# Seven-product gated feed-forward: a PSUM copy put ahead of three activations, and further buffers for weights and their sums

## The chip, the cores and the metric

The kernel runs on one core of a Trainium2 chip. The metric is device time in microseconds of one execution, and less is better. The times of the kernel before are 1887.44, 1888.04 and 1890.42 us, median 1888.04 us.

## What the kernel computes

The reference is one hybrid decoder block over 1024 tokens of width 1024, in float32. Two token mixers (an RWKV-7 recurrence and a retention) run first; then comes the gated feed-forward, which is the part that the change touches:

```
def conv_ffn(h, w_up, conv_w, conv_b, w_down):
    u = h @ w_up                                  # 1024 -> 2 * 2816
    up = jnp.pad(u, ((0, 0), (CONV_WIDTH - 1, 0), (0, 0)))
    u = sum(up[:, i:i + T] * conv_w[i] for i in range(CONV_WIDTH)) + conv_b
    gate, val = jnp.split(u, 2, axis=-1)
    return (jax.nn.gelu(gate, approximate=True) * val) @ w_down
```

## The kernel before

Everything lies transposed, channels on the 128 partitions and tokens along the free dimension, in two halves of 512 tokens. The 2816 gate channels and the 2816 value channels are 22 pairs of tiles of 128. Every float32 product is made of three TensorE passes over operands split in a high and a low part (`mm3`, L224 to L226).

The first three pairs are done in the usual way (`up_std`). The other 19, the loop over `n`, use a scheme of seven products instead of eight: sums and differences of weight quarters (`sa`, and `st1`, `st2` written over) times sums of activations prepared before (`T1` to `T4`). For n below 4 (`NEAR`) two of the seven products were made earlier and come by DMA; from n = 4 on all seven are made in the loop, in TensorE's order: first half of the first product (X1, into `pX`), Z1 (`pZ`), T1 (`pT`), Y (`pY`), second half of the first product onto the same bank (X2), Z2 onto `pZ`, T2 onto `pT`. Each is four tiles by three passes, 12 matmuls, so 84 an iteration. Below, X1, X2 and so on mean these products; the order on TensorE runs across iterations, so that X1, Z1, T1 and Y of the next iteration stand behind X2, Z2, T2 of this one.

ACT copies X1 out of `pX` into `s1` (L1188), and X2 must wait for that, because it accumulates on the same bank. Other results: L1193 copies Z1 to `s5`, DVE adds T1 and Y (L1195, L1197), ACT copies X2 (L1200), POOL adds `s1` and `s5` (L1201), DVE adds Z2 and T2 (L1203, L1205). They fill `ub[0]` (gate channels) and `ub[1]` (value channels), each with two token halves.

Then `conv` runs four times an iteration (two tiles, two halves): one ACT activation (L1065) and two DVE operations with three operands (L1066, L1068). `gate` runs twice: a gelu on ACT (L1073), a DVE product (L1074), and a store to `f_d` issued from ACT's queue (L1075), which stands in that queue until the product is done.

The weights of an iteration: two loads from SP's queue (L1150, L1153) into `st1` and `st2`, each of two buffers that alternate; DVE makes `sa` in its single buffer (L1168, L1169) and two more differences in place (L1171, L1172); `cut` casts to the high part on ACT (L1164) and subtracts for the low part on POOL or DVE (L1165): for `w1`, `w2`, and both halves of `w3` on POOL, for half of `w4` on DVE. This code stands under a priority of 500 instructions, so it runs ahead of the products it serves.

A scheduler at compile time fixes each engine's order from a simulated timeline, by data readiness and program order, which `tc.high_priority(offset=...)` moves forward by so many instructions. On the chip every engine takes its list in order and waits on semaphores.

Of the kernel before, what the change touches and what calls it, by code (L numbers as in the profile page):

```python
# [9 lines left out]
F32 = mybir.dt.float32  # L10
F32R = mybir.dt.float32r
I32 = mybir.dt.int32
AF = mybir.ActivationFunctionType
# [15 lines left out]
E05 = math.exp(-0.5)  # L29
TWO_PI = 2.0 * math.pi  # L30
WPRIO = 500
MAGIC = 12582912.0
C1 = 6.25
C2 = 0.033203125
# [124 lines left out]
def body(tc, nc, xT, xN, pos, wch, wbrw, wbret, wout, wup, wdn, w2a2, gw2, rows, vecs, consts0, consts1, out):  # L159
    V, S, G, PE = nc.vector, nc.scalar, nc.gpsimd, nc.tensor  # L160
    ctx = ExitStack()

    @contextmanager
    def tile_pool(**kw):
        with tc.tile_pool(**kw) as pool:
            yield Lines(pool)

    with ctx:
# [7 lines left out]
        wp = ctx.enter_context(tile_pool(name="wp", bufs=3, reuse_waits="tile"))  # L176
# [25 lines left out]
        def load_w(src, kt, full=None, hi=None, lo=None, st=None, eng=None):  # L202

            wp, nb = wpools[cnt[0] % len(wpools)]
            with tc.high_priority(offset=WPRIO if cnt[0] > 3 else 0):
                if st is None:
                    st = wp.tile([128, full or kt, 128], F32, tag="ws", name="w_st", bufs=nb[0])[:, 0:kt, :]
                nc.sync.dma_start(st, src)
            with tc.high_priority(offset=WPRIO if cnt[0] > 1 else 0):
                if hi is None:  # L210
# [55 lines left out]
        ws = pz.tile([128, 2, KT, 128], F32, tag="ARp", name="w_sx")  # L266
        wx = pz.tile([128, 2, KT, 128], F32R, tag="BKp", name="w_x")
# [7 lines left out]
        with tile_pool(name="x0", bufs=2, reuse_waits="tile") as xp:  # L275
# [22 lines left out]
            for q in range(NJ):  # L298
                xn = xp.tile([128, D], F32, tag="xn", name="xn", bufs=3)
                nc.sync.dma_start(xn, xN[128 * q:128 * q + 128, :])  # L300
                S.activation(xn, xn, AF.Square, accum_out=rsm[:, q:q + 1])
            with tc.high_priority(offset=WPRIO):
                V.tensor_scalar(rsm[:, 8:16], rsm[:, 0:8], 1.0 / D, RMS_EPS, ALU.mult, ALU.add)
# [24 lines left out]
        with pctx, tile_pool(name="p1", bufs=1, reuse_waits="tile", side="right") as p1:  # L328
# [159 lines left out]
            n = gp.tile([128, 512], F32, tag="rt", name="nrot", bufs=1)  # L488
            V.tensor_scalar(n, ang, 1.0 / TWO_PI, C("turn"), ALU.mult, ALU.add)
            V.tensor_scalar(n, n, MAGIC, MAGIC, ALU.add, ALU.subtract)  # L490
            for c_ in (C1, C2, C3):
# [14 lines left out]
        def qk_pair(m):  # L506

            ws = [load_w(wch[14 + 2 * m + e], 8) for e in range(2)]
            for hf in range(2):
                h_ = slice(hf * 512, (hf + 1) * 512)  # L510
                ab = []
                for e in range(2):
                    ps = psA.tile([128, 512], F32, tag="a", name="ps_side")
                    proj(ws[e], ps, hf)
                    with tc.high_priority(offset=WPRIO):
                        t = gp.tile([128, 512], F32, tag=f"qk{e}", name="qk", bufs=1)
# [17 lines left out]
        def side_tile(i):  # L534

            w = load_w(wch[i], 8)
            for hf in range(2):
                ps = psA.tile([128, 512], F32, tag="a", name="ps_side")
                proj(w, ps, hf)
                with tc.high_priority(offset=WPRIO):  # L540
                    ot = gp.tile([128, 512], F32, tag="ot", name="ot")
# [237 lines left out]
        def first_stage(j):  # L779

            nonlocal R
            tk = slice(j * 128, (j + 1) * 128)
            with tc.high_priority(offset=WPRIO):
                zvg = t2.tile([128, 24, 128], F32, name="zvg")
# [181 lines left out]
        with (tile_pool(name="mg", bufs=2, reuse_waits="tile") as mp,  # L966
              tile_pool(name="mg2", bufs=1, reuse_waits="tile") as mp2):
            for hf in range(2):
# [43 lines left out]
                for cs_ in ((0, 1),) + tuple((c,) for c in range(2, 8)):  # L1012

                    ws = [load_w(wout[c], 8) for c in cs_]
# [30 lines left out]
        w3s = w3ctx.enter_context(tile_pool(name="w3s", bufs=1, reuse_waits="tile"))  # L1045
# [15 lines left out]
        def conv(pool, ub, b, j, src):  # L1061

            i = j + FT * b
            u = pool.tile([128, 512], F32, tag=f"u{b}", name="u_f")
            S.activation(u, src, AF.Identity, bias=VC("cb")[:, i:i + 1], scale=VC("cw2")[:, i:i + 1])  # L1065
            V.scalar_tensor_tensor(out=u, in0=ub[:, 1:513], scalar=VC("cw1")[:, i:i + 1], in1=u,  # L1066
                                   op0=ALU.mult, op1=ALU.add)
            V.scalar_tensor_tensor(out=u, in0=ub[:, 0:512], scalar=VC("cw0")[:, i:i + 1], in1=u,  # L1068
                                   op0=ALU.mult, op1=ALU.add)
            return u  # L1070

        def gate(j, hf, u0, u1):
            S.activation(u0, u0, AF.Gelu_apprx_tanh)  # L1073
            V.tensor_tensor(out=u0, in0=u0, in1=u1, op=ALU.mult)  # L1074
            nc.scalar.dma_start(f_d[hf, j], u0)  # L1075

# [33 lines left out]
        for n0 in range(0, NEAR, 2):  # L1110
            ws = [load_w(wup[NSTD + n], 8) for n in (n0, n0 + 1)]
# [27 lines left out]
        wx = ctx.enter_context(tile_pool(name="wx", bufs=1, reuse_waits="tile", side="right"))  # L1139
# [3 lines left out]
        fp = fctx.enter_context(tile_pool(name="fp", bufs=2, reuse_waits="tile"))  # L1143
        W8 = [128, 8, 128]
        lh, rh_ = slice(0, 4), slice(4, 8)

        for n, j in enumerate(range(NSTD, FT)):
            with tc.high_priority(offset=WPRIO):
                st1 = wp.tile(W8, F32, tag="ws", name="w_st", bufs=2)
                nc.sync.dma_start(st1, wup[j])  # L1150

                st2 = wx.tile(W8, F32, tag="ws", name="w_st", bufs=2) if n else w3s.tile(W8, F32, tag="ws", name="w_st")
                nc.sync.dma_start(st2, wup[j + FT])  # L1153
                sa = wx.tile(W8, F32, tag="sa", name="w_sa") if n else w3s.tile(W8, F32, tag="wh", name="w_sa")
                if n >= NEAR:
                    w1 = wp.tile(W8, F32R, tag="wh", name="w_hi", bufs=3), wx.tile(W8, F32R, tag="wl", name="w_lo", bufs=3)
                wh = (wx, 2) if n else (wp, 3)
                w2 = (wh[0].tile(W8, F32R, tag="wh", name="w_hi", bufs=wh[1]),
                      wx.tile(W8, F32R, tag="wl", name="w_lo", bufs=3) if n else w3s.tile(W8, F32R, tag="wl", name="w_lo"))
                w3 = wp.tile(W8, F32R, tag="wh", name="w_hi", bufs=3), wp.tile(W8, F32R, tag="wl", name="w_lo", bufs=2)  # L1160
                w4 = wh[0].tile(W8, F32R, tag="wh", name="w_hi", bufs=wh[1]), wp.tile(W8, F32R, tag="wl", name="w_lo", bufs=2)

                def cut(w, ks, src, eng):
                    S.copy(w[0][:, ks, :], src)  # L1164
                    eng.tensor_tensor(out=w[1][:, ks, :], in0=src, in1=w[0][:, ks, :], op=ALU.subtract)  # L1165
                if n >= NEAR:
                    cut(w1, slice(0, 8), st1, G)
                V.tensor_tensor(out=sa[:, lh, :], in0=st2[:, lh, :], in1=st2[:, rh_, :], op=ALU.add)  # L1168
                V.tensor_tensor(out=sa[:, rh_, :], in0=st1[:, lh, :], in1=st2[:, lh, :], op=ALU.subtract)  # L1169
                cut(w2, slice(0, 8), sa, G)  # L1170
                V.tensor_tensor(out=st2[:, lh, :], in0=sa[:, lh, :], in1=st1[:, lh, :], op=ALU.subtract)  # L1171
                V.tensor_tensor(out=st1[:, rh_, :], in0=st1[:, rh_, :], in1=st2[:, lh, :], op=ALU.subtract)  # L1172
                cut(w3, lh, st2[:, lh, :], G)
                cut(w3, rh_, st1[:, rh_, :], G)
                cut(w4, lh, st2[:, rh_, :], V)
            if n >= NEAR:
                pX = psA.tile([128, 512], F32, tag="a", name="ps_x")
            pZ = bank("ps_z", "B")
            pT = bank("ps_t", "CY"[n % 2])
            pY = bank("ps_y", "AI"[n % 2])  # L1180
            ub = [fp.tile([128, 1026], F32, tag=f"ub{b}", name="ub") for b in range(2)]
            for b in range(2):
                G.memset(ub[b][:, 0:2], 0.0)
            s1 = fp.tile([128, 512], F32, name="s1")
            s5 = fp.tile([128, 512], F32, name="s5")
            if n >= NEAR:
                mmb(pX, w1, range(4), hn2[0][0:4], True, True)
                S.copy(s1, pX)  # L1188
            else:
                nc.sync.dma_start(s1, e_d[n, 0])  # L1190
                nc.sync.dma_start(ub[0][:, 2:514], e_d[n, 1])
            mmb(pZ, w2, range(4), T1, True, True)
            S.copy(s5, pZ)  # L1193
            mmb(pT, w2, range(4, 8), T3, True, True)
            V.tensor_tensor(out=s5, in0=pT, in1=s5, op=ALU.add)  # L1195
            mmb(pY, w3, range(4), T2, True, True)
            V.tensor_tensor(out=s1, in0=pY, in1=s1, op=ALU.add)  # L1197
            if n >= NEAR:
                mmb(pX, w1, range(4, 8), hn2[0][4:8], False, True)
                S.copy(ub[0][:, 2:514], pX)  # L1200
            G.tensor_tensor(out=ub[1][:, 514:1026], in0=s1, in1=s5, op=ALU.add)  # L1201
            mmb(pZ, w3, range(4, 8), hn2[1][4:8], False, True)
            V.tensor_tensor(out=ub[0][:, 514:1026], in0=pZ, in1=s1, op=ALU.add)  # L1203
            mmb(pT, w4, range(4), T4, False, True)
            V.tensor_tensor(out=ub[1][:, 2:514], in0=pT, in1=s1, op=ALU.add)  # L1205
            for hf in range(2):
                cv = [conv(fp, ub[b][:, 512 * hf:512 * hf + 514], b, j, ub[b][:, 512 * hf + 2:512 * hf + 514])
                      for b in range(2)]
                gate(j, hf, *cv)
        fctx.close()  # L1210
        w3ctx.close()

# [68 lines left out]
        for c in range(8):  # L1281
# [5 lines left out]
            ws = [load_w(wdn[c][:, k0:k0 + kn, :], kn, full=8) for k0, kn in ((0, 8), (8, 8), (16, 6))]  # L1287
# [28 lines left out]
```

## Time and profile before

| quantity | value |
|---|---|
| median of three runs | 1888.04 us |
| the profiled execution's own time | 1895.04 us |
| its span | 1893.2 us |
| TensorE busy, share of the span | 94% |
| DVE, ACT, POOL busy | 62%, 34%, 36% |
| mean granted TensorE clock | 0.982 |
| iterations n = 4 to 18, from the first X2 to the last | 1322.53 to 1609.74 us |

The profile comes from one execution, with times from the start of its span. A busy time counts what an engine executes, also while an instruction stands blocked inside it; "idle before" is the time in which the engine waited ahead of an instruction, with the instruction that released it.

### The profile page before, as it was taken

Reading aid. Unit: us, or ns where it says so; the run is one execution under the profiler, and the core shown is the slowest. Engines: PE = TensorE matmul, PEld = TensorE weight load, DVE = VectorE, ACT = ScalarE, POOL = GpSimd, SP = SyncE. Lnnn points to the kernel's source line nnn. Section 1 sums busy time; section 2 is a strip of 40 time slices with the busy share of each in tenths; the row PEclk is TensorE's granted clock in tenths of the full one; section 3 lists DMA queues with packets and bytes.
Section 4 is the critical chain, followed back from the end, with each engine's and each line's share of the span. In section 5 each row is a group of like instructions: output and inputs, shape, how many; then the busy total and the mean of one; then the engine's idle time right before and its main releaser. Section 6 shows DMA issues by size and latency. Waiting matters only on the chain.

```text
span 1893.2 us, 27391 instructions
## 1 busy us (share of the span) xinstructions
PE 1786.2 (94%) x10610; PEld 1448.0 (76%) x10610; DVE 1182.6 (62%) x2068; ACT 649.9 (34%) x993; POOL 687.0 (36%) x491
## 2 busy tenths in 40 slices
PE   8779999999999999999999999888999999989996
PEld 7667778788777788888788778676777777868885
DVE  4786584755666634663444837789888887753413
ACT  6543211111111113322343435544434444443320
POOL 1344523311122122111463744554554454222523
PEclk9989999999999999999999999999999999999998
DMA  8233532433423225555653835433222222665531
GB/s 287 86 114 100 186 86 70 134 90 89 115 88 115 72 84 159 176 178 167 205 167 102 261 116 168 167 117 99 85 78 72 86 69 88 218 205 144 188 92 45
DMA packets 202690, 244.44 MB, mean 129 GB/s; under 512 B 60992, under 2 KB 136256, under 8 KB 201536
## 3 DMA queue, kind: packets, MB, share of 16 engines
q1 hardware_dynamic: 125712, 171.11, 29.8%
q10 hardware_dynamic: 76848, 71.59, 11.6%
q8 instruction: 83, 1.36, 0.3%
q14 instruction: 47, 0.39, 0.1%
HBM read 177.10 MB, written 65.54 MB: 128 GB/s over the span
## 4 chain that ended last, share of the span: by engine, by line
PE 53%; DVE 18%; DMA 8%; issue 4%; POOL 3%; ACT 3%; ACTq 0%; SPq 0%; DVEq 0%; POOLq 0%
PE ps_side L225 7%; PE ps_side L224 7%; PE ps_side L226 7%; DVE u_f L1066 4%; PE ps_dn L226 3%; PE ps_dn L225 3%; PE ps_dn L224 3%; DMA w_st<-in_wup_dram 2%; DVE u_f L1068 2%; POOL w_lo L1165 2%; DVE w_sa L1169 2%; PE ps_o L225 1%; PE ps_o L226 1%; PE ps_o L224 1%; DVE w_sa L1168 1%
## 5 line engine op out<-in xcount | busy, mean ns | idle before, releaser
L218 POOL TENSOR_TENSOR w_lo<-w_st,w_hi 128x1024 fp32r<-128x1024 f32 (+2 forms) x111 | 259.8, 2341 | 515.7 <-ACT w_hi L212 183.5
L212 ACT CAST w_hi<-w_st 128x1024 fp32r<-128x1024 f32 (+2 forms) x162 | 161.7, 999 | 412.6 <-PE ps_side L225 130.7
L225 PE MATMUL ps_side<-hnl,w_hi 128*128 128x512 f32 x640 | 256.2, 400 | 0.0
L224 PE MATMUL ps_side<-hnh,w_hi 128*128 128x512 f32 x640 | 255.6, 399 | 0.0
L226 PE MATMUL ps_side<-hnh,w_lo 128*128 128x512 f32 x640 | 254.9, 398 | 0.0
L224 PEld LDWEIGHTS ps_side<-hnh,w_hi 128*128 128x128 f32 x640 | 121.0, 189 | 26.9 <-issue 1.5
L225 PEld LDWEIGHTS ps_side<-hnl,w_hi 128*128 128x128 f32 x640 | 121.0, 189 | 26.5 <-issue 1.5
L226 PEld LDWEIGHTS ps_side<-hnh,w_lo 128*128 128x128 f32 x640 | 121.1, 189 | 26.3 <-issue 0.8
L218 DVE TENSOR_TENSOR w_lo<-w_st,w_hi 128x1024 fp32r<-128x1024 f32 (+1 forms) x51 | 65.2, 1279 | 82.3 <-ACT w_hi L212 40.6
L1066 DVE SCALAR_TENSOR_TENSOR u_f<-ub,vct,u_f 128x512 f32<-128x512 f32 x88 | 102.1, 1164 | 13.2 <-ACT u_f L1065 11.5
L1165 POOL TENSOR_TENSOR w_lo<-w_st,w_hi 128x512 fp32r<-128x512 f32 (+1 forms) x53 | 105.5, 2012 | 3.8 <-ACT w_hi L1164 2.3
L1065 ACT ACTIVATE u_f<-ub,vct 128x512 f32<-128x512 f32 x76 | 59.8, 812 | 124.4 <-DVE ub L1203 99.2
L224 PE MATMUL ps_rw<-hnh,w_hi 128*128 128x512 f32 (+1 forms) x224 | 87.7, 392 | 13.1 <-ACT hnh L289 6.8
L225 PE MATMUL ps_rw<-hnl,w_hi 128*128 128x512 f32 (+1 forms) x224 | 86.7, 387 | 0.5 <-DVE hnl L290 0.5
L226 PE MATMUL ps_rw<-hnh,w_lo 128*128 128x512 f32 (+1 forms) x208 | 80.0, 385 | 0.0
L226 PE MATMUL ps_b<-y_hi,w_lo 128*128 128x512 f32 x192 | 75.2, 392 | 2.8 <-DVE w_lo L218 1.8
L1068 DVE SCALAR_TENSOR_TENSOR u_f<-ub,vct,u_f 128x512 f32<-128x512 f32 x88 | 76.9, 892 | 0.2
L224 PE MATMUL ps_b<-y_hi,w_hi 128*128 128x512 f32 x192 | 75.2, 392 | 0.7 <-ACT w_hi L212 0.6
L225 PE MATMUL ps_b<-y_lo,w_hi 128*128 128x512 f32 x192 | 74.9, 390 | 0.0
L224 PE MATMUL ps_dn<-f_k,w_hi 128*128 128x512 f32 (+1 forms) x198 | 72.4, 366 | 0.0
L226 PE MATMUL ps_dn<-f_k,w_lo 128*128 128x512 f32 (+1 forms) x198 | 72.4, 366 | 0.0
L225 PE MATMUL ps_dn<-f_k,w_hi 128*128 128x512 f32 (+1 forms) x198 | 72.2, 366 | 0.0
(418 smaller groups left out, 4346.6 us busy)
## 6 DMA issues: line engine op xcount, KB each, us to landing
w_st<-in_wup_dram SPq DMA_DIRECT2D x54, 512.0 KB, 3.5
w_st<-in_wch_dram SPq DMA_DIRECT2D x52, 512.0 KB, 3.9
w_st<-in_wdn_dram SPq DMA_DIRECT2D x38, 512.0 KB, 4.0
pj_d<-ot ACTq DMA_DIRECT2D x64, 256.0 KB, 2.2
zvg<-pj_d SPq DMA_DIRECT2D x8, 1536.0 KB, 8.9
f_d<-u_f ACTq DMA_DIRECT2D x44, 256.0 KB, 2.1
L<-L_d SPq DMA_DIRECT2D x8, 1344.0 KB, 5.9
w_st<-in_wbret_dram SPq DMA_DIRECT2D x16, 512.0 KB, 3.9
```

The costliest lines, as they stand in the source:

```text
L212: S.copy(hi, st)
L218: eng.tensor_tensor(out=lo, in0=st, in1=hi, op=ALU.subtract)
L224: PE.matmul(ps, wh, xh, start=first and a == 0, stop=False, skip_group_check=skip)
L225: PE.matmul(ps, wh, xl, start=False, stop=False, skip_group_check=skip)
L226: PE.matmul(ps, wl, xh, start=False, stop=last and a == n - 1, skip_group_check=skip)
L1065: S.activation(u, src, AF.Identity, bias=VC("cb")[:, i:i + 1], scale=VC("cw2")[:, i:i + 1])
L1066: V.scalar_tensor_tensor(out=u, in0=ub[:, 1:513], scalar=VC("cw1")[:, i:i + 1], in1=u, op0=ALU.mult, op1=ALU.add)
L1068: V.scalar_tensor_tensor(out=u, in0=ub[:, 0:512], scalar=VC("cw0")[:, i:i + 1], in1=u, op0=ALU.mult, op1=ALU.add)
L1165: eng.tensor_tensor(out=w[1][:, ks, :], in0=src, in1=w[0][:, ks, :], op=ALU.subtract)
L1168: V.tensor_tensor(out=sa[:, lh, :], in0=st2[:, lh, :], in1=st2[:, rh_, :], op=ALU.add)
L1169: V.tensor_tensor(out=sa[:, rh_, :], in0=st1[:, lh, :], in1=st2[:, lh, :], op=ALU.subtract)
```

## The change

Two things change in the loop over `n`. First, buffers that the first stage of the feed-forward left free (the pool `w3s`) are used again: `st1` and `st2` take every third iteration's tile from there, so each rotates over three buffers, and `sa` alternates between two. Second, an iteration's last work is cut out into a function, `rest`: `conv` of both halves of the value tile, the gelu of the second half of the gate tile, both products and both stores. It is called in the next iteration, right behind the copy of X1 (for n of 4 and above), with `tc.issue_after`, which holds the block's ACT instructions behind that copy in ACT's list, and with a priority of 40. `conv` of both halves of the gate tile and the gelu of the first half stay where they were.

```
-                st1 = wp.tile(W8, F32, tag="ws", name="w_st", bufs=2)
+                st1 = (wp.tile(W8, F32, tag="ws", name="w_st", bufs=2) if n % 3 or not n else
+                       w3s.tile(W8, F32, tag="wl", name="w_st"))
...
-                st2 = wx.tile(W8, F32, tag="ws", name="w_st", bufs=2) if n else w3s.tile(W8, F32, tag="ws", name="w_st")
+                st2 = (wx.tile(W8, F32, tag="ws", name="w_st", bufs=2) if n % 3 else
+                       w3s.tile(W8, F32, tag="ws", name="w_st"))
...
-                sa = wx.tile(W8, F32, tag="sa", name="w_sa") if n else w3s.tile(W8, F32, tag="wh", name="w_sa")
+                sa = wx.tile(W8, F32, tag="sa", name="w_sa") if n % 2 else w3s.tile(W8, F32, tag="wh", name="w_sa")
...
                 mmb(pX, w1, range(4), hn2[0][0:4], True, True)
-                S.copy(s1, pX)
+                c1 = S.copy(s1, pX)
+                with tc.issue_after(c1.ins), tc.high_priority(offset=GPRIO):
+                    rest()
             else:
+                rest()
                 nc.sync.dma_start(s1, e_d[n, 0])
...
-            for hf in range(2):
-                cv = [conv(fp, ub[b][:, 512 * hf:512 * hf + 514], b, j, ub[b][:, 512 * hf + 2:512 * hf + 514])
-                      for b in range(2)]
-                gate(j, hf, *cv)
+            def part(b, hf, j=j, ub=ub):
+                return conv(fp, ub[b][:, 512 * hf:512 * hf + 514], b, j, ub[b][:, 512 * hf + 2:512 * hf + 514])
+            u0 = [part(0, hf) for hf in range(2)]
+            S.activation(u0[0], u0[0], AF.Gelu_apprx_tanh)
+            def rest(j=j, part=part, u0=u0):
+                gate(j, 0, u0[0], part(1, 0), gelu=False)
+                gate(j, 1, u0[1], part(1, 1))
+        rest()
```

## Rows read from the trace of the kernel before

**Rows 1.** Windows, twelve iterations: length, busy us of PE, PEld, DVE, ACT, POOL, clock, DMA.
```profile
1343.49:1589.81 246.32, 232.18 (x1009) 188.28 (x1009) 209.57 (x229) 110.08 (x169) 120.67 (x84) 1.00 0.24 77
```

**Rows 2.** The waits of PE from 1240 to 1660 us: us in total, times, longest.
```profile
PE ps_x L224 <- ACT s L1188: 18.4, 15, 2.5
PE ps_z L224 <- ACT s L1193: 3.3, 1, 3.3
```

**Rows 3.** The timeline of PE: start, us, what, [idle before <-releaser]; single matmuls.
```profile
1322.53 0.50 PE L224 MATMUL ps_x<-b_hi,w_hi 128*128 128x512 f32 x1 [2.51 <-ACT s L1188]
...
1410.57 0.39 PE L224 MATMUL ps_t<-b_hi,w_hi 128*128 128x512 f32 x1
...
1419.41 0.39 PE L224 MATMUL ps_t<-b_hi,w_hi 128*128 128x512 f32 x1
...
1609.74 0.50 PE L224 MATMUL ps_x<-b_hi,w_hi 128*128 128x512 f32 x1 [0.56 <-ACT s L1188]
```

**Rows 4.** The timeline of ACT through one iteration.
```profile
1400.17 0.81 ACT L1065 ACTIVATE u_f<-ub,vct 128x512 f32<-128x512 f32 x1 [7.81 <-DVE ub L1203]
...
1402.41 1.52 ACT L1065 ACTIVATE u_f<-ub,vct 128x512 f32<-128x512 f32 x2 [0.39 <-DVE ub L1205]
1403.84 0.61 ACT L1073 ACTIVATE u_f<-u_f 128x512 f32<-128x512 f32 x1
1404.36 0.56 ACT L1188 COPY s<-ps_x 128x512 f32<-128x512 f32 x1
...
1408.67 1.05 ACT L1164 CAST w_hi<-w_sa 128x1024 fp32r<-128x1024 f32 x1 [3.26 <-DVE u_f L1074]
```

**Rows 5.** The timeline of DVE through the same iteration.
```profile
1399.46 0.68 DVE L1203 TENSOR_TENSOR ub<-ps_z,s 128x512 f32<-128x512 f32 x1
...
1405.48 1.41 DVE L1068 SCALAR_TENSOR_TENSOR u_f<-ub,vct,u_f 128x512 f32<-128x512 f32 x2
...
1406.80 1.29 DVE L1074 TENSOR_TENSOR u_f<-u_f 128x512 f32<-128x512 f32 x2
...
1408.01 0.69 DVE L1195 TENSOR_TENSOR s<-ps_t,s 128x512 f32<-128x512 f32 x1
...
1408.61 0.69 DVE L1197 TENSOR_TENSOR s<-ps_y,s 128x512 f32<-128x512 f32 x1
...
1412.24 1.76 DVE L1168 TENSOR_TENSOR w_sa<-w_st 128x512 f32<-128x512 f32 x1 [2.95 <-POOL w_lo L1165]
...
1417.32 2.88 DVE L1066 SCALAR_TENSOR_TENSOR u_f<-ub,vct,u_f 128x512 f32<-128x512 f32 x1
1420.12 0.68 DVE L1203 TENSOR_TENSOR ub<-ps_z,s 128x512 f32<-128x512 f32 x1
```

**Rows 6.** The timeline of POOL through the same iteration.
```profile
1409.80 2.41 POOL L1165 TENSOR_TENSOR w_lo<-w_sa,w_hi 128x1024 fp32r<-128x1024 f32 x1 [2.69 <-ACT w_hi L1164]
1412.16 1.29 POOL L1201 TENSOR_TENSOR ub<-s,s 128x512 f32<-128x512 f32 x1
1413.41 6.24 POOL L1165 TENSOR_TENSOR w_lo<-w_st,w_hi 128x512 fp32r<-128x512 f32 x3
```

**Rows 7.** The timeline of DVE and POOL around 1318 us.
```profile
1317.60 0.68 DVE L1203 TENSOR_TENSOR ub<-ps_z,s 128x512 f32<-128x512 f32 x1
1318.20 2.35 DVE L1066 SCALAR_TENSOR_TENSOR u_f<-ub,vct,u_f 128x512 f32<-128x512 f32 x1
...
1317.58 2.42 POOL L1165 TENSOR_TENSOR w_lo<-w_st,w_hi 128x1024 fp32r<-128x1024 f32 x1 [0.46 <-ACT w_hi L1164]
```

**Rows 8.** The load of `st2`: SP's queue, and the issues from 1343 to 1590 us (median us to landing).
```profile
1403.67 0.33 SPq L1153 DMA_DIRECT2D w_st<-in_wup_dram  x1
...
w_st<-in_wup_dram SPq DMA_DIRECT2D x22, 512.0 KB, 3.5
```

**Rows 9.** The timeline of PE: the first use of the low part of `w2`.
```profile
1416.46 0.39 PE L226 MATMUL ps_z<-b_hi,w_lo 128*128 128x512 f32 x1
```

More of the change, by code (lines that the diff above doesn't have):

```diff
@@ L31 @@
 WPRIO = 500
+GPRIO = 40
 MAGIC = 12582912.0
@@ L1070, in conv, with gate @@
             return u
-        def gate(j, hf, u0, u1):
-            S.activation(u0, u0, AF.Gelu_apprx_tanh)
+        def gate(j, hf, u0, u1, gelu=True):
+            if gelu:
+                S.activation(u0, u0, AF.Gelu_apprx_tanh)
             V.tensor_tensor(out=u0, in0=u0, in1=u1, op=ALU.mult)
@@ L1145, in body, with rest @@
         lh, rh_ = slice(0, 4), slice(4, 8)
+        def rest():
+            pass
         for n, j in enumerate(range(NSTD, FT)):
             with tc.high_priority(offset=WPRIO):
-                st1 = wp.tile(W8, F32, tag="ws", name="w_st", bufs=2)
+                st1 = (wp.tile(W8, F32, tag="ws", name="w_st", bufs=2) if n % 3 or not n else
+                       w3s.tile(W8, F32, tag="wl", name="w_st"))
                 nc.sync.dma_start(st1, wup[j])
-                st2 = wx.tile(W8, F32, tag="ws", name="w_st", bufs=2) if n else w3s.tile(W8, F32, tag="ws", name="w_st")
+                st2 = (wx.tile(W8, F32, tag="ws", name="w_st", bufs=2) if n % 3 else
+                       w3s.tile(W8, F32, tag="ws", name="w_st"))
                 nc.sync.dma_start(st2, wup[j + FT])
-                sa = wx.tile(W8, F32, tag="sa", name="w_sa") if n else w3s.tile(W8, F32, tag="wh", name="w_sa")
+                sa = wx.tile(W8, F32, tag="sa", name="w_sa") if n % 2 else w3s.tile(W8, F32, tag="wh", name="w_sa")
                 if n >= NEAR:
```

## The prediction

> **What bounds the kernel now.** I read the page's slices first (TensorE busy 94% of the span), then the loop that the diff touches, by windows, by TensorE's waits and by the timelines of the four engines. In twelve steady iterations TensorE is busy 232.18 of 246.32 us at a granted clock of 1.00, the upper of its two levels, DVE 209.57, POOL 120.67, ACT 110.08 [rows 1]. One wait stands out: X2 waits for ACT's copy of X1 in all 15 iterations, 18.4 us [rows 2].
>
> How much that costs is better read from starts. From the first X2 to the last there are 14 iterations in 1609.74 - 1322.53 = 287.21 us, 20.52 each; the window of rows 1 runs from one X2 to the X2 twelve iterations on, 246.32 / 12 = 20.53 [rows 1, 3]. Matmuls without a wait start 8.84 us apart over 39 steps, 0.2267 each, so 84 of them take 19.04 us [rows 3]. An iteration thus loses 1.49 us, and at most 14 x 1.48 = 20.7 us can be had here.
>
> What sets 20.53? Not TensorE: X1 was complete long before its copy started at 1404.36. In ACT's list that copy stands behind the activation that waits 7.81 us for DVE's L1203, a gelu, and then three more, from 1402.41 to 1404.36 [rows 4]. L1203 itself had its product long before; DVE came to it late. Following DVE backwards from L1203 at 1420.12: 2.88 us of L1066 and, from 1412.24 to 1417.32, three sums of weights, and ahead of these 2.95 us of waiting for POOL, because `sa` has one buffer and POOL still reads it [rows 5]. POOL's piece, 2.41 us from 1409.80, waited for ACT's cast at 1408.67 [rows 4, 6]; ACT stood in front of that cast until DVE's L1074, since the stores to `f_d` wait in ACT's list; L1074 follows the convolutions, and these follow L1203 of the iteration before. The circle L1203, activation, convolutions, L1074, store, cast, POOL, sums, L1066, L1203 closes in 20.66 us here (L1203 at 1399.46 and at 1420.12 [rows 5]) and holds no product of TensorE. TensorE idles because it is the faster of the two.
>
> **The change part by part.**
>
> *The copy ahead of three activations.* It could start when the cast ahead of 1402.41 is done, some 2.3 us earlier than 1404.36 (two activations of 1.52 us together, the gelu, and the 0.39 us of waiting [rows 4]). TensorE's gap is 1.49, so this covers it once. But it only moves the copy inside the circle: with the circle at 20.53 TensorE would win 1.49 us once and then wait again. By itself I count this part at 1.5 us in total. Its cost is 0.56 us of ACT ahead of the activations of the value tile, of which 0.39 us is cover (they waited for L1205); without that cover the circle is 0.56 us longer. No work is added: the three activations, four convolution steps on DVE, two products and two stores are the same ones. What is moved past: the stores remain on ACT's queue behind the copy; SP's queue is passed by nothing.
>
> *Two buffers for `sa`.* This cuts the circle at the wait of 2.95 us (33 to 34 us over twelve iterations). DVE can go from L1197 at 1408.61 straight to the sums. What is late next is the pair DVE and POOL: the sums run at 1.76 us beside POOL, though DVE's operations on two arrays do 0.60 to 0.66 us when alone (from starts: L1068 twice in 1.32, L1074 twice in 1.21, L1195 to L1197 0.60) [rows 5], and POOL's three pieces need 6.24 us [rows 6] where, by half of 2.41 for each half-size piece, 4.8 would do. L1066 at 1318.20 ends 2.35 us later with POOL's piece, while L1203, which reads one array from PSUM, takes 0.68 us beside the same piece [rows 7]. So the two take turns, and only operations with a PSUM input run beside POOL.
>
> This gives a budget for one iteration: DVE has 15 operations that exclude POOL, 8 x 0.66 + 7 x 0.60 = 9.5 us; POOL has 2 x 2.41 + 2 x 1.2 + 1.29 = 8.5 us; together 18.0 us. The four PSUM additions are 4 x 0.60 = 2.4 us. Now they all lie outside POOL's time: 18.0 + 2.4 = 20.4, and measured is 20.53, so the budget accounts for the period. After the change POOL no longer has to be through before L1203, so L1203 and L1205 can run beside it: 20.53 - 1.2 = 19.3 us, and with all four beside it 18.1, which is below TensorE's 19.04. The bounds of the new period are therefore 19.04 and 20.53; I take 19.25, between 19.04 and 19.3 plus some unused turns, because two of the four additions come free in any order.
>
> The Trainium skill ("SBUF — State Buffer", section Who interferes with whom) says that DVE with two SBUF inputs and a reading GpSimd exclude each other, whoever issued first holding the port for the whole instruction, and that one SBUF input does not contend. The trace agrees: 2.88 and 2.35 against 0.66 us, and 0.68 us for the PSUM form. Without this rule, DVE would have only its 12 us of work, and the sum would be 14 x 1.48 = 20.7 instead of 17.8.
>
> *Three buffers for `st1` and `st2`.* The load of `st2` is issued at 1403.67 and lands 3.5 us later, at 1407.2, which is 2.0 us before DVE is through with L1197 at 1409.2 [rows 5, 8]. Today the wait on `sa` covers it; once DVE comes to the sums more than 2.0 us earlier, it is next. The third buffer puts the load an iteration earlier. Gain by itself 0; without it up to 2.95 - 2.0 = 0.95 us an iteration of the gain on `sa` would be at risk. The number of loads and their queue are the same, DMA is at 0.24.
>
> *The first iterations.* The 3.3 us wait for L1193 and the excess of the first X2 wait (2.51) lie outside the 14 periods [rows 2, 3]. They hang on the same engines in a different order; bounds 0 and 5.8, taken 2, as the copy there was already ahead of two activations and only earlier sums help. It could be negative by the 0.56 us of the copy.
>
> *Sum.* 287.21 - 14 x 19.25 = 17.7, plus 2: 19.7 us. The profiled execution took 1895.04 us (span 1893.2), so 1875.3 by its own time; the median of the runs is 7.0 us less, and a saving counted on the timeline is carried over whole: 1868.3 us.
>
> **The rivals.**
>
> *The turns stay tight (20%).* DVE and POOL pack worse than I assume, since POOL's pieces come in one row behind the casts and DVE's convolutions stand blocked behind them. For it: 18.0 us of exclusive work in 19.04 leaves only 1.0 us for everything else. Against it: nothing forces POOL's row to end before L1203 any more. Period 19.6 to 20.3: gain 3 to 13 us, 1875 to 1885. The rule of the Trainium skill named above ("SBUF — State Buffer", Who interferes with whom), read strictly, speaks for this rival.
>
> *The circle merely changes its route (12%).* ACT's cast of `sa` still stands behind the stores, and the stores behind L1074; if the compile-time order puts the sums back behind the same piece of POOL, the period stays near 20.5 and only the copy's 1.5 us come: 1886.5.
>
> *Slower (10%).* With free buffers and a priority of 500 the three sums may be placed ahead of L1074 on DVE. They cost 1412.24 to 1417.32, 5.1 us, when POOL runs; L1074, both stores, ACT's cast and POOL's low part of `w2` come that much later. That part is done at 1412.2 and first used at 1416.46 [rows 9], 4.2 us of slack. It decides from 4.2 us on: at 5.1 plus the copy's 0.56, TensorE stands 1.5 us before Z1 while the circle is no shorter, half of it made up by the earlier sums: 14 x 0.5 = 7, 1895. Against it: in the steady order POOL is idle when the sums would run early, and then they take 1.8 us in all.
>
> **How the numbers follow.** My forecast, with a period of 19.04 to 19.6, has 55% and gives 1861 to 1874; a larger gain (first iterations in full, and the end of the loop) 3%. With the rivals above: faster 55 + 20 + 3 = 78%, within 0.2% (about 3.8 us, what a measurement of this kernel can tell from no change) 12%, slower 10%. The range 1860 to 1887 leaves out the slower case, the far half of the unchanged one and the 3%: under two in ten. The predicted time is 1868.
>
> **What would show it.** Right: X2 starts about 19.25 us apart, the wait of L1168 for POOL gone, the copy directly behind the gelu of the first half and its wait under 5 us over 15 iterations, L1203 or L1205 beside a piece of POOL. The turns: X2 apart by 19.6 or more with more DVE operations of 1.7 us and above. Unchanged: a new releaser of 2 us or so ahead of the sums. Slower: the sums ahead of L1074, and TensorE waiting for L1165 or L1164 before Z1. My forecast fails if TensorE waits an iteration for anything other than the copy by more than 0.5 us.

## The result, and the profile after

The changed kernel takes 1878.39 us, median of 7 runs (1873.41 to 1882.48), beside 1890.42 us for the kernel before in the same session (7 runs, 1887.40 to 1895.29): a ratio of 0.9934 (95% interval [0.9917, 0.9951]), 12 us less. The forecast was 1868, 20 us less.

| profiled execution | before | after |
|---|---|---|
| its own time, us | 1895.04 | 1882.48 |
| span, us | 1893.2 | 1880.7 |
| first product of the loop n = 0 (Z1) to the first X2 (n = 4) | 83.36 | 85.10 |
| 14 iterations, n = 4 to 18, from X2 to X2 | 287.21 | 277.43 |
| from the X2 of n = 18 to the end | 283.46 | 277.63 |
| one steady iteration | 20.53 | 19.88 |

Of the 12.5 us of span, the loop gives 9.8 and the stretch behind it 5.8; the loop's first iterations lose 1.7 and the work ahead of the loop 1.4. Line numbers after are higher than before: L1188 is L1197, L1195 is L1207, L1203 is L1215, L1066 is L1067, L1074 is L1076, L1075 is L1077, L1164 and L1165 are L1171 and L1172, L1168 is L1175.

The first three rows of before have these answers. First the windows of after over ten steady iterations (columns as in [rows 1]):

```profile
1370.29:1569.12 198.83, 194.24 (x840) 156.11 (x840) 174.57 (x191) 90.83 (x141) 100.52 (x70) 1.00 0.24 77
```

198.83 / 10 = 19.88 us an iteration. TensorE still idles 0.46 us in each. The waits of TensorE in after from 1230 to 1660 us (in total, times, longest):

```profile
PE ps_z L225 <- ACT s L1205: 5.5, 1, 5.5
PE ps_t L225 <- DVE s L1207: 5.0, 11, 0.5
...
PE ps_x L225 <- ACT s L1197: 1.7, 2, 0.9
```

The wait of X2 for the copy of X1 (18.4 us in 15, [rows 2]) is down to 1.7 us in 2. In its place T2, which goes onto T1's bank, waits for DVE's addition of T1 (L1207) in 11 iterations. The timeline of TensorE in after, that wait and the two ends of the 14 iterations (columns as in [rows 3]):

```profile
1325.64 0.50 PE L225 MATMUL ps_x<-b_hi,w_hi 128*128 128x512 f32 x1 [0.83 <-ACT s L1197]
...
1429.10 0.39 PE L227 MATMUL ps_z<-b_hi,w_lo 128*128 128x512 f32 x1
1429.94 0.50 PE L225 MATMUL ps_t<-b_hi,w_hi 128*128 128x512 f32 x1 [0.45 <-DVE s L1207]
1430.28 0.39 PE L226 MATMUL ps_t<-b_lo,w_hi 128*128 128x512 f32 x1
...
1603.07 0.39 PE L225 MATMUL ps_x<-b_hi,w_hi 128*128 128x512 f32 x1
```

Why T1's addition is late is told by the chain of waits in after, one turn of it (start, us, what):

```profile
1440.62 0.61 DVE ub L1215
...
1441.25 0.83 ACT u_f L1066
...
1442.10 0.75 DVE u_f L1067
...
1445.31 1.32 DVE u_f L1067 x2
1446.64 1.32 DVE u_f L1069 x2
1447.96 0.61 DVE u_f L1076
...
1448.60 0.33 ACTq L1077
...
1448.97 1.06 ACT w_hi L1171
...
1450.09 2.41 POOL w_lo L1172
...
1452.52 1.77 DVE w_sa L1175
1454.30 1.70 DVE w_sa L1176
...
1457.61 2.88 DVE u_f L1067
1460.49 0.61 DVE ub L1215
```

This is the circle that the prediction read out of [rows 4 to 6], closed in 1460.49 - 1440.62 = 19.87 us, and no product of TensorE is in it. It should have been cut between POOL's piece and the sum of L1175 and was not. One thing in it is new: only one of DVE's two products (0.61 of the 1.28 us of L1076) stands ahead of the store and the cast. ACT's timeline in after shows why; below it stand DVE's products, its wait ahead of the sums, and POOL's next pieces:

```profile
1448.60 0.33 ACTq L1077 DMA_DIRECT2D f_d<-u_f  x1
1448.97 1.05 ACT L1171 CAST w_hi<-w_sa 128x1024 fp32r<-128x1024 f32 x1 [2.96 <-DVE u_f L1076]
1449.20 0.33 ACTq L1077 DMA_DIRECT2D f_d<-u_f  x1
...
1447.89 1.28 DVE L1076 TENSOR_TENSOR u_f<-u_f 128x512 f32<-128x512 f32 x2
...
1452.52 1.77 DVE L1175 TENSOR_TENSOR w_sa<-w_st 128x512 f32<-128x512 f32 x1 [2.16 <-POOL w_lo L1172]
...
1453.71 6.23 POOL L1172 TENSOR_TENSOR w_lo<-w_st,w_hi 128x512 fp32r<-128x512 f32 x3
```

In before both stores stand ahead of the cast at 1408.67 [rows 4]. ACT's timeline:

```profile
1407.53 1.10 ACTq L1075 DMA_DIRECT2D f_d<-u_f  x2
```

In after the cast of `sa` stands between the two stores; in before it stands behind both, and so behind both products. That is 0.6 us off the circle, and 20.53 - 19.88 = 0.65 is what an iteration gained. The rest of the circle is as long as it was. From L1203 (L1215 in after) to the first product takes 7.34 us in before [rows 5] and, in the chain of after, 7.34 us; from the cast to the sums takes 3.57 and 3.55. The starts of the first product and of the cast lie 1.08 us apart in after, and in before 1.69 in most iterations (1.87 in the one of [rows 4, 5]).

The compile-time order explains the 2.16 us that stayed. In before the sums for iteration n + 2 stand on DVE behind Y's addition of iteration n; in after it is those for n + 3 (counted in DVE's list). With further buffers for `sa`, `st1` and `st2` the order of the sums ran one iteration further ahead, and the buffer that a sum writes is again the one that POOL has just begun to read.

### The profile page after: what moved, and what is told of

It is laid out like the page before. It is cut to its first block, busy times and chain, and to the rows that moved or that the text cites. A ratio compares the mean times of both kernels' runs of the same rounds, so it can differ in the third digit from the quotient of the medians.

```text
span 1880.7 us, 27396 instructions
## 1 busy us (share of the span) xinstructions
PE 1788.1 (95%) x10610; PEld 1450.5 (77%) x10610; DVE 1177.7 (63%) x2068; ACT 648.9 (35%) x993; POOL 687.7 (37%) x491
## 4 chain that ended last, share of the span: by engine, by line
PE 51%; DVE 20%; DMA 8%; issue 5%; POOL 3%; ACT 3%; ACTq 0%; SPq 0%; DVEq 0%; POOLq 0%
PE ps_side L225 7%; PE ps_side L226 7%; PE ps_side L227 7%; DVE u_f L1067 4%; PE ps_dn L227 3%; PE ps_dn L226 3%; PE ps_dn L225 3%; DVE u_f L1069 3%; POOL w_lo L1172 2%; PE ps_o L226 1%; PE ps_o L227 1%; PE ps_o L225 1%; DVE w_sa L1176 1%; DVE xprod L629 1%; PE ps_b L227 1%
## 5 line engine op out<-in xcount | busy, mean ns | idle before, releaser
L1067 DVE SCALAR_TENSOR_TENSOR u_f<-ub,vct,u_f 128x512 f32<-128x512 f32 x88 | 102.6, 1183 | 15.0 <-ACT u_f L1066 15.0
L1172 POOL TENSOR_TENSOR w_lo<-w_st,w_hi 128x512 fp32r<-128x512 f32 (+1 forms) x53 | 106.2, 2026 | 4.1 <-ACT w_hi L1171 3.0
L1066 ACT ACTIVATE u_f<-ub,vct 128x512 f32<-128x512 f32 x76 | 59.9, 813 | 101.3 <-DVE ub L1215 93.9
```

## Experiments

Three accounts were open: the circle through cast, POOL and sums sets the period; or the turns that DVE and POOL take do; or each half of the change did what it was made for and the two do not add up. Medians below are against the kernel before on the same chip: 1891.94 us for the first four (13 runs), 1890.58 for the others (11 runs). Windows and waits are of 1400 to 1560 us, and the 14 iterations those of the table above.

**e1_rest_only: the change without its buffers.**

```
-                st1 = (wp.tile(..., bufs=2) if n % 3 or not n else w3s.tile(...))
+                st1 = wp.tile(W8, F32, tag="ws", name="w_st", bufs=2)
...
-                sa = wx.tile(..., tag="sa") if n % 2 else w3s.tile(..., tag="wh")
+                sa = wx.tile(..., tag="sa") if n else w3s.tile(..., tag="wh")
```

> The change without its buffers: one sa buffer, two buffers each for st1 and st2, but the copy of X1 ahead of three activations and the deferred rest as in the change. Theory A (the gain of the changed kernel, 19.88 us an iteration against 20.53, comes from ACT's order alone: the cast of sa now stands between the two stores and no longer behind both, so the circle is shorter by one product of 0.6 us; the second sa buffer only lets the sums run three iterations ahead instead of two and their wait for POOL stays): 19.9 us an iteration, the wait of the sums for POOL still 2.2 us, time like the changed kernel, 1876 to 1881, some 12 us under the kernel before. Rival B (the buffers carry the gain): 20.5 us, 1887 to 1891.

Measured 1881.5 us, 0.9949 [0.9936, 0.9961], half a microsecond above the expected 1876 to 1881; 278.17 us for the 14 iterations, period 19.87. DVE's wait ahead of the sums (in total, times, longest), e1:

```profile
DVE w_sa L1173 <- POOL w_lo L1170: 17.3, 8, 2.2
```

It is the same wait, 17.3 us in 8, and the same period as in after. So the whole gain of the loop's steady part belongs to the moved block, and the buffers give it nothing. In e1, too, the cast stands between the two stores.

**e2_buffers_only: the buffers without the moved block.**

```
-                sa = wx.tile(..., tag="sa") if n else w3s.tile(..., tag="wh")
+                sa = wx.tile(..., tag="sa") if n % 2 else w3s.tile(..., tag="wh")
```

(and the lines of `st1` and `st2` as in the change)

> The change's buffers alone: two for sa, three each for st1 and st2; the copy of X1 and the last activations as before. Theory A (the extra buffers are used up by running ahead): 20.5 us an iteration, the sums still wait 2.9 us for POOL, time as before, within 4 us. Rival B (a second sa buffer cuts the wait): the wait gone, 19.3 to 19.9 us, 9 to 17 us faster than before.

Measured 1887.18 us, 0.9975 [0.9965, 0.9985]: a gain of 4.8 us by the medians, a little over the 4 expected, with the period of before (20.52). DVE's wait in e2:

```profile
DVE w_sa L1170 <- POOL w_lo L1167: 22.4, 8, 3.0
```

Before has 22.5 us in 8 there, so all three buffers together move nothing in the steady loop. Of the span's 7.8 us, 1.5 lie in the loop, 1.0 in the first iterations and 6.9 behind n = 18, against 1.7 lost ahead of the loop.

**e3_stores_on_sp: the change, with the loop's stores to `f_d` issued from SP's queue.** If the circle decides, the cast must not stand behind a store that waits for a product.

```
-            nc.scalar.dma_start(f_d[hf, j], u0)
+            (nc.sync if j >= NSTD else nc.scalar).dma_start(f_d[hf, j], u0)
```

> The changed kernel with the stores of the loop issued from SP's queue, so ACT no longer stands in front of a store until DVE's product is done. Theory A (circle through store, cast, POOL, sums): ACT's wait of 2.96 us ahead of the cast of sa goes, POOL's first piece starts some 3 us earlier, the wait of the sums for POOL (2.16 us) goes, and the iteration falls from 19.88 to between 19.04 (TensorE alone) and 19.4 us: 7 to 13 us faster than the changed kernel, about 1866 to 1872. Rival C (DVE and POOL take turns on SBUF and are full at 19.9 us): POOL's earlier pieces only push the convolutions back, 19.7 to 19.9 us, within 3 us of the changed kernel. Rival D (SP's weight loads get stuck behind the stores): a wait of the sums for a load, slower than the changed kernel.

Measured 1866.24 us, 0.9861 [0.9846, 0.9876]. The windows of e3, then the cast and POOL's piece in its timelines:

```profile
1400.00:1560.00 160.00, 160.00 (x707) 132.56 (x707) 144.61 (x161) 76.50 (x118) 93.73 (x61) 1.00 0.25 84
```

```profile
1456.54 1.06 ACT L1171 CAST w_hi<-w_sa 128x1024 fp32r<-128x1024 f32 x1
...
1474.89 0.57 ACT L1205 COPY s<-ps_z 128x512 f32<-128x512 f32 x1
1475.36 1.05 ACT L1171 CAST w_hi<-w_sa 128x1024 fp32r<-128x1024 f32 x1
...
1477.65 3.23 POOL L1172 TENSOR_TENSOR w_lo<-w_sa,w_hi 128x1024 fp32r<-128x1024 f32 x1
...
1480.92 1.76 DVE L1175 TENSOR_TENSOR w_sa<-w_st 128x512 f32<-128x512 f32 x1 [1.10 <-POOL w_lo L1172]
```

The cast follows the copy with no wait, where after has 2.96 us. TensorE has no idle time in 160 us, and the period is 19.04, which is its own 84 x 0.2267 [rows 3]. The sums still wait 1.10 us for POOL and cost nothing: the circle is still closed, now through ACT's own run of activations and copies, but one turn of it takes 18.82 us (the cast at 1456.54 and at 1475.36), 0.2 us less than TensorE needs. No sum waits for a load.

**e4_sums_held: the change, with the two sums of `sa` held behind Y's addition of the iteration two earlier.** This keeps the further buffers and takes away the run-ahead.

```
+                with tc.issue_after(ys[n - 2].ins) if n - 2 >= NEAR else nullcontext():
                     V.tensor_tensor(out=sa[:, lh, :], ...)
...
-            V.tensor_tensor(out=s1, in0=pY, in1=s1, op=ALU.add)
+            ys.append(V.tensor_tensor(out=s1, in0=pY, in1=s1, op=ALU.add))
```

> The changed kernel with the two sums of weights kept to two iterations ahead (put behind Y's addition of that iteration in DVE's order), so that with two sa buffers they wait for no POOL semaphore. Theory A1 (the wait on the sa buffer is what closes the circle): the 2.16 us of idle ahead of the first sum go, the iteration falls to 19.0 to 19.4 us, 7 to 12 us faster than the changed kernel. Theory A2 (POOL's piece, started 0.2 us earlier, excludes the sum anyway): the idle time turns into a longer first sum, from 1.77 to 2.5 us and more, and the iteration stays at 19.7 to 19.9 us, within 3 us of the changed kernel.

Measured 1872.98 us, 0.9898 [0.9884, 0.9911]; 266.56 us for the 14 iterations. The period is the expected one, but the time is 5.4 us under the changed kernel by the medians (6.8 by the ratios), where 7 to 12 were expected. What e4 loses against e3 lies ahead of the 14 iterations: the first X2 starts at 1328.46 us, in e3 at 1322.84, behind a wait for ACT's copy of Z1 that takes 6.1 us here and 3.5 in e3. The windows of e4, then DVE and POOL in its timelines:

```profile
1400.00:1560.00 160.00, 160.00 (x708) 132.55 (x707) 159.72 (x165) 80.24 (x120) 85.83 (x60) 1.00 0.25 83
```

```profile
1463.04 0.67 DVE L1212 TENSOR_TENSOR s<-ps_y,s 128x512 f32<-128x512 f32 x1
1463.63 2.75 DVE L1178 TENSOR_TENSOR w_sa<-w_st 128x512 f32<-128x512 f32 x1
...
1463.43 2.41 POOL L1174 TENSOR_TENSOR w_lo<-w_sa,w_hi 128x1024 fp32r<-128x1024 f32 x1 [1.92 <-ACT w_hi L1173]
```

The sum now starts 0.2 us after POOL's piece instead of behind it: with the lead back at two iterations the second buffer does what it is for. The sum takes 2.75 us instead of 1.77, as the two take turns, and DVE is busy 159.72 of 160 us with no idle time to be seen. Yet TensorE is full and the period is 19.04: much of that busy time is time blocked inside an instruction, and the turns, as tight as before, no longer set the period. The room is small: DVE's first sums are 18.76 us apart (1463.63 and 1482.39), 0.3 us less than TensorE's 19.04.

**e5_sp_and_held: e3 and e4 together.** Its edit is the two diffs above.

> Both single cures at once: stores on SP's queue and the sums held to two iterations ahead. If the loop's limit is now TensorE's own 19.04 us an iteration (the theory of the circle), nothing is left to win in the loop: 19.04, time within 4 us of the kernel with the stores on SP (1866). If something else still cost time inside the loop there, it would fall below that.

Measured 1867.09 us, 0.9873 [0.9852, 0.9895], the same 19.04 and 266.56 us. In the loop the two cures take away the same loss; either alone is enough.

**e6_second_sa_only: the kernel before, with a second buffer for `sa` and nothing else.** If the third buffers of `st1` and `st2` feed the run-ahead, the circle should open without them.

```
-                sa = wx.tile(..., tag="sa") if n else w3s.tile(..., tag="wh")
+                sa = wx.tile(..., tag="sa") if n % 2 else w3s.tile(..., tag="wh")
```

> The kernel before with the second sa buffer alone (two buffers each for st1 and st2, the copy of X1 where it was). In DVE's order the sums now wait for the load alone and no longer for POOL, since two buffers for st2 hold them to two iterations ahead; they stand ahead of the two products of the gate. Theory A (the circle): the wait for POOL is gone and the iteration falls from 20.53 to 19.04 to 19.6 us, 10 to 22 us under the kernel before: the third buffers of the change undid the second sa buffer. Rival (my slow case: the sums ahead of the products delay stores, cast and POOL's low part of w2): TensorE waits before Z1 and the iteration stays at 20.0 us or above. Rival (the turns of DVE and POOL): 19.7 to 20.2.

Measured 1874.02 us, 0.9914 [0.9892, 0.9936]; period 19.04. The windows of e6, then DVE's timeline at the sums:

```profile
1400.00:1560.00 160.00, 160.00 (x708) 132.48 (x707) 127.08 (x162) 80.33 (x116) 80.57 (x59) 1.00 0.26 85
```

```profile
1477.04 0.69 DVE L1168 TENSOR_TENSOR w_sa<-w_st 128x512 f32<-128x512 f32 x1 [0.32 <-DMA w_st<-in_wup_dram]
1477.65 0.69 DVE L1169 TENSOR_TENSOR w_sa<-w_st 128x512 f32<-128x512 f32 x1
1478.25 1.29 DVE L1074 TENSOR_TENSOR u_f<-u_f 128x512 f32<-128x512 f32 x2
...
1480.47 2.40 POOL L1165 TENSOR_TENSOR w_lo<-w_sa,w_hi 128x1024 fp32r<-128x1024 f32 x1 [3.53 <-ACT w_hi L1164]
```

One line, without the moved block, takes the loop from 287.21 to 269.40 us. With two buffers each for `st1` and `st2` the loads hold the sums back (they now wait for a load, 0.32 us here), and the two sums of `sa` stand ahead of the products of L1074, 3.4 us ahead of POOL's piece, at 0.69 us each. The only difference to e2 is the third buffers: in e2 these undid the second `sa`.

**e8_third_u0: e3, with a third buffer for the gate tile `u_f`.** e3's first iterations show TensorE waiting once for L1205 (3.5 us), behind an activation that waits 8.12 us for a store of `f_d` to read its buffer out.

```
-            u = pool.tile([128, 512], F32, tag=f"u{b}", name="u_f")
+            u = pool.tile([128, 512], F32, tag=f"u{b}", name="u_f", **({"bufs": 3} if j >= NSTD and not b else {}))
```

> The changed kernel with the stores on SP and a third buffer for the gate tile u0 in the loop. In the first iterations ACT stands 8.1 us in front of an activation whose u0 buffer waits for its store; with a third buffer this should go, the 3.5 us of TensorE's wait before Z1 of iteration 4 with it: 2 to 4 us less than the kernel with the stores on SP. The period stays 19.04. If TensorE's wait there comes from the weights and not from ACT, nothing changes.

Measured 1870.26 us, 0.9893 [0.9873, 0.9913]: no gain over e3. ACT's timeline in e8 at that place:

```profile
1298.13 0.63 ACT L1223 ACTIVATE u_f<-u_f 128x512 f32<-128x512 f32 x1 [8.59 <-DVE u_f L1069]
```

The wait for the store is gone, and a wait of 8.59 us for DVE stands in its place; TensorE's wait is 4.0 us. A miss: the wait for the store was not the only one ACT meets there.

**e9_before_stores_on_sp: the kernel before, with only the stores moved to SP's queue.** The edit is e3's line.

> The kernel before with nothing changed but the stores of the loop, from SP's queue. Theory A (the circle through store, cast, POOL, sums is what sets the period): ACT's 3.3 us in front of the cast go, POOL starts earlier, the iteration falls from 20.53 to 19.04 to 19.4 us although the copy of X1 still stands behind three activations: 15 to 22 us under the kernel before. Rival (the place of the copy costs TensorE's wait): the iteration falls by no more than half and X2 still waits 0.7 us and more for the copy.

Measured 1867.96 us, 0.9879 [0.9856, 0.9903]; period 19.04, 268.12 us for the 14 iterations. The windows of e9 and its ACT timeline:

```profile
1400.00:1560.00 160.00, 160.00 (x707) 132.48 (x707) 144.23 (x162) 81.66 (x121) 91.11 (x61) 1.00 0.25 82
```

```profile
1470.07 0.58 ACT L1193 COPY s<-ps_z 128x512 f32<-128x512 f32 x1
1470.54 1.06 ACT L1164 CAST w_hi<-w_sa 128x1024 fp32r<-128x1024 f32 x1
```

One line, with one buffer for `sa` and the copy of X1 where it was, gives 22.6 us by the medians, just over the expected 15 to 22 and about twice what the whole change gives. e3, e5 and e9 have overlapping intervals; all three beat both kernels.

## Why the prediction was right and where it was wrong

**What bounds the kernel: right.** The circle through DVE, ACT and POOL set 20.53 us, and TensorE idled because it was faster. Shortened at three different places (store: e3, e9; lead of the sums: e4; buffer: e6), it lets the period fall to 19.04 each time, TensorE's own. One thing in the profile could be read otherwise. In most turns the chain of waits in before goes through the load of `st2`:

```profile
1403.67 3.46 DMA w_st<-in_wup_dram
...
1407.18 0.02 DVEq L1168
...
1407.40 0.70 DVE u_f L1074
```

But DVE works without a gap up to 1407.40, so the load is no later than DVE is; and e9, with two buffers for `st2` as in before, runs at 19.04.

**The copy ahead of three activations: right in kind, wrong in sum.** The copy alone only moved TensorE's wait, from X2 to T2. But the block that moved with it was counted at 1.5 us, and e1 shows 9.0 in the 14 iterations. I wrote that the two stores stay on ACT's queue behind the copy, and did not ask on which side of them the cast of `sa` comes out. It came out between them, worth 0.6 us an iteration.

**Two buffers for `sa` cut the circle: the step that failed.** This was the main term (33 to 34 us of waiting cut, 17.7 us of loop). In the change the wait did not go: it is 2.16 us instead of 2.95 and still on the circle; e2 shows that the buffers alone leave the period as it was. In itself the step was sound: e6 is that edit alone, and its loop is 17.8 us shorter, where 17.7 were put on it. That the two agree so closely is luck: the period there is 19.04, not 19.25, and 2.8 us are lost again in the first of the 14 iterations. I took the number of buffers for the distance between writer and reader. The order of the sums is made at compile time, and it used the buffers to run ahead. So the 1878 us lie inside the stated 1860 to 1887 by luck: that the time came out faster was due to the place of the cast, to which the sum gave nothing, and to the stretch behind the loop.

**Three buffers for `st1` and `st2`: wrong sign.** Counted at nothing, with 0.95 us an iteration at risk without them. Without them (e6) the sums wait at most 0.7 us for the load and the loop is full; with them (e2) the run-ahead came back. The 2.0 us of room for the load were also too many: in the chain above, the wait for it (L1168) stands ahead of the second product in DVE's list, with 0.2 us to spare.

**The budget of turns: it fitted by accident.** 18.0 + 2.4 = 20.4 us met the measured 20.53, and the period was taken as 19.25 from it. e4 runs at 19.04 with DVE busy 159.72 of 160 us, e6 at 19.04 with 127.08. The exclusion is there (2.75 us beside POOL, 0.69 without), but how much of it is met depends on the order, and a sum of busy times did not give the period of any of these kernels. What is met does lengthen the circle: in before, three sums from 1412.24 to 1417.32 and L1066 to 1420.12 take 7.9 us [rows 5], where by the prediction's own 0.60 and 0.66 us 2.5 would do; so about 5.4 us of a turn are, by this estimate, time blocked by POOL. The two additions that were to run beside POOL in the changed kernel do not: L1067 (2.88 us), ahead of L1215 in DVE's list, is held until POOL's row ends (1453.71 + 6.23 = 1459.94), and L1215 starts after that. The 12 us measured lie in the range of the rival of the turns, and the period of 19.88 in its 19.6 to 20.3; the mechanism is that of the other rival, the circle that changes its route.

**The slower rival: its mechanism came, its price did not.** In e6 the two sums of `sa` do stand ahead of L1074. POOL being idle then, they start 0.6 us apart, as the prediction's counter-argument said, and in the steady loop TensorE waits for nothing.

**The rest of the sum.** The first iterations were put at a gain of 2 and lost 1.7: TensorE waits 5.5 us for L1205 where it waited 3.3 us for L1193 [rows 2]. The stretch behind n = 18 was put at nothing and gave 5.8. Kernels with all the further buffers have 276.5 to 277.6 us there (e8 280.4), those without 278.2 to 283.5, and TensorE's wait there for DVE's low parts is 3.4 us in after, 5.8 in before. Whether the buffers cause this or two single profiles differ by chance is not settled. So the sum was 17.7 + 2 + 0 where the profile has 9.8 - 1.7 + 5.8, less 1.4 ahead of the loop.

**The test set for failure was set too high.** I wrote that the forecast fails if TensorE waits over 0.5 us an iteration for anything but the copy. It waits 0.41 to 0.48 (for DVE's L1207), and the period is 19.88 - 19.04 = 0.84 above its own: a short wait costs more than its idle time. In before it was 1.49 lost for 1.18 idle (246.32 - 232.18 over twelve iterations, [rows 1]). The starts show it: the first matmul behind the wait in after comes 0.84 us after the one ahead of it (1429.10 to 1429.94) and the second another 0.34, where 0.23 each is usual. The profile counts idle time only from the end of the matmul ahead, 0.39 us behind its start, while without a wait the next one starts 0.23 us behind it.

## What to carry to other kernels

A loop can be bound by a circle of waits through engines of which none is full: follow the latest wait backwards until it meets itself one iteration on, and list every edge; then cut the edge that is cheapest to cut, which here was a store that stood in ACT's list ahead of a cast. A further buffer shortens such a circle only if the order of issue does not use it up, so look at which iteration's tile the writer fills, and hold the writer's lead (e4) or add one buffer at a time (e6). A budget of busy times that adds up to the period proves nothing while one of its engines is seen to wait.

## What the runs showed of the hardware

A store in ACT's queue holds the whole list behind it until its data is ready: 2.96 us ahead of each cast of `sa` in after, 3.26 in before [rows 4]. In e3 and e9 no cast of `sa` waits for a store; the stores wait in SP's queue instead, 40.0 us in all between 1400 and 1560 us in e3 and 30.5 in e9.

An instruction's busy time holds its blocked time: DVE shows 159.72 us busy of 160 in e4 and 127.08 in e6 at the same period; among other things the same sum takes 2.75 us when POOL's piece was issued first, ending 0.5 us behind it, and 0.69 us when POOL is idle. The Trainium skill ("SBUF — State Buffer", section Who interferes with whom) says that such a pair excludes each other and that the first issued holds the port to its end; these rows agree.
